# Differential heads' halves in their own 64 rows, scores in three products of 64 rows each

## The chip, the core and the metric

The kernel runs on one core of one Trainium2 chip. The metric is the device time of one execution in microseconds (us); the time of before is the median of three runs. The profile is one further execution, recorded by the hardware profiler. Engines are named as in the profile: PE is TensorE's matrix products and PEld its weight loads, DVE is VectorE, ACT ScalarE, POOL GpSimd, and SP SyncE, which issues most transfers.

## What is computed

Two layers of a mixer with three head groups in parallel. The part that the change touches is the scores of group D, differential attention: 6 heads, each with two halves of 64 dimensions, whose softmaxes are subtracted. Cut to that:

```python
SEQ, DIFF_HEADS, DIFF_HALF_DIM, DIFF_V_DIM = 256, 6, 64, 128
...
h = rmsnorm(x, norm_g[l])
proj = h @ w_in[l]
a_x, a_b, a_c, a_g, d_q, d_k, d_v, d_g, m_q, m_g = jnp.split(proj, offsets, axis=-1)
...
q = rmsnorm(d_q.reshape(b, s, DIFF_HEADS, 2, DIFF_HALF_DIM), diff_q_norm_g[l])
k = rmsnorm(d_k.reshape(b, s, DIFF_HEADS, 2, DIFF_HALF_DIM), diff_k_norm_g[l])
...
sc = jnp.einsum('bhcqd,bhckd->bhcqk', qi, kt).astype(jnp.float32) * scale + bias[None, :, None]
p = jax.nn.softmax(sc, axis=-1).astype(vt.dtype)
o = jnp.einsum('bhcqk,bhkd->bhcqd', p, vt)
return o[:, :, 0] - lam.astype(o.dtype) * o[:, :, 1]
...
x = x + jnp.concatenate([y_a, y_d, y_m], axis=-1) @ w_out[l]
```

All inputs and the output are float32.

## The kernel before

Precision first. A large product is made of three products in fp32r: each operand is split into an upper part `hi` (rounded to fp32r) and a lower part `lo` (the rest), and hi·hi, hi·lo and lo·hi are summed in PSUM (L304, L305, L306). Weights come in by transfers of 128 × 1024 (`raw`), ACT makes `hi` (L283), and DVE makes `lo` (L284). The activations of a layer, 256 tokens, stand with the dimension on the 128 rows, in `xT` for the input projection and in `yT` for the output projection; `yT` has 2 parts × 16 slices of 256 tokens, and its slices are also used, before the output projection needs them, for queries and keys.

A layer is a row of blocks: `block` (L287 on) runs over 16 slices of the contraction in chunks of two, for 512 columns and two groups of 128 tokens, so a chunk has 12 products of 512 columns. After each chunk `run_side` moves forward the other work of the layer: tasks, written as generators, that fall due by chunk numbers. The attention's heads run there, in pairs (`pair`), one pair every nine chunks. Which instruction stands where on an engine follows from this program order and from a planner that simulates the engines when the program is built; `pin` (`keep_in_program_order`) holds the written order for an instruction.

A head of group D goes through these steps. `normed` normalizes queries and keys by token; `turn_sheet` transposes them (by 32 × 32 blocks on DVE, then through DRAM), so that `whole` has for each head a slice of 256 tokens with its first half in rows 0 to 63 and the second in rows 64 to 127. `qk_T` (from L457) splits them. For each half `c`, `own` are its own 64 rows and `other` the other 64:

- the query slice of a half, `yT[:, c, h]`, gets the upper part in `own` (L469) and the lower part in `other` (L470);
- the first key slice gets the upper part in both (L481, L482); the second gets the lower part in `own` (L486) and a copy of it in `other` (L488). For heads 4 and 5 this second slice lies in a tile of its own, `k2`.

So one product of 128 rows (L544) sums hi·hi and lo·hi, and a second (L545) sums hi·lo and lo·lo. `diff_scores` (from L537) makes 8 products of 256 columns a head: two halves, two groups of 128 queries, two products. The two halves' scores go to two PSUM tiles, `s[0]` and `s[1]`; the pool `ps_s` has two buffers. DVE reads them at L549 (adding the distance bias), then come the maximum (L551), the exponential on ACT (L555), and the difference of both halves (L562). Group M's scores (`mem_scores`, L590) and the products of probabilities with values (`weighted`, L437) are f32 products of 128 rows.

Two more instructions on PE matter below. Small vectors are turned at the start: `va` (32 rows, L817) and `vb` (64 rows, L145), each by one transposition between products of the memory projection (L738). Token blocks `xs` are turned by transpositions of 128 rows (L716), two at a time.

Of the kernel before, what the change touches and what calls it, by code (L numbers as in the profile page):

```python
# [11 lines left out]
F32 = mybir.dt.float32  # L12
# [36 lines left out]
def encoder(ctx: ExitStack, tc: tile.TileContext, x, mem, norm_g, w_in, conv_w, conv_b,  # L49
# [21 lines left out]
    def nm(s):  # L71
        uid[0] += 1
        return f"{s}_{uid[0]}"
# [369 lines left out]

    def q_parts(yT, c, h):
        return yT[:, c, h, :]

    def k_first(yT, c, h):
        return yT[:, c, CG + h, :]  # L450

    def k_second(yT, k2, c, h):
        return yT[:, c, CG + DH + h, :] if h < 4 else k2[:, c, h - 4, :]

    ROWS = (slice(0, HALF), slice(HALF, P))

    def qk_T(l, yT, k2, nat, q, k):  # L457

        whole = yield from turn_sheet(nat)

        pin = tc.keep_in_program_order
        if q is not None:
            c0, h0, nh = q
            a = c0 // P
            for c in range(2):
                own, other = ROWS[c], ROWS[1 - c]
                src = whole[own, a:a + nh, :]
                hi = yT[own, c, h0:h0 + nh, :]
                pin(nc.scalar.copy(hi, src))  # L469
                pin(nc.vector.tensor_tensor(yT[other, c, h0:h0 + nh, :], src, hi.bitcast(F32), ALU.subtract))  # L470
                yield
            made.update(("q", l, h) for h in range(h0, h0 + nh))
        if k is not None:
            c0, h0, nh = k
            a = c0 // P
            for c in range(2):
                own, other = ROWS[c], ROWS[1 - c]
                src = whole[own, a:a + nh, :]
                g = kgain[own, l:l + 1]
                hi = yT[own, c, CG + h0:CG + h0 + nh, :]  # L480
                pin(nc.scalar.activation(hi, src, AF.Copy, scale=g))  # L481
                pin(nc.scalar.activation(yT[other, c, CG + h0:CG + h0 + nh, :], src, AF.Copy, scale=g))  # L482
                for at, n, dst, d0 in ((0, min(nh, 4 - h0), yT, CG + DH + h0), (4 - h0, h0 + nh - 4, k2, 0)):
                    if n > 0:
                        lo = dst[own, c, d0:d0 + n, :]
                        pin(nc.vector.scalar_tensor_tensor(lo, whole[own, a + at:a + at + n, :], g,  # L486
                                                           hi[:, at:at + n].bitcast(F32), ALU.mult, ALU.subtract))
                        pin(nc.scalar.copy(dst[other, c, d0:d0 + n, :], lo))  # L488
                yield
            made.update(("k", l, h) for h in range(h0, h0 + nh))  # L490

    scored = set()
# [3 lines left out]
    def pair(heads, begin, end, v):  # L496

        es = []
        for h in heads:
            while held["e"] == 2:  # L500
                yield 1
            held["e"] += 1
            es.append((yield from begin(h)))
            yield 2
        yield 4
        while held["sh"] == 2:
            yield 1
        held["sh"] += 1
        sh = tmp.tile([P, NA, 2, NT * NT, B], F32, tag="sh", name=nm("sh"))
        for i, e in enumerate(es):  # L510
            tc.keep_in_program_order(nc.vector.transpose(
                sh[:, :, i], e[0].rearrange("p t (k b c) -> p b (t k) c", k=NT, b=NA)))
            held["e"] -= 1
            yield 1
        yield 4
        flat = sh.rearrange("p b h n c -> p (b h n c)")
        yield from carry(sh.rearrange("p b h n c -> p b (h n c)"), flat.rearrange("p (n a i) -> p n a i", a=NA, i=B))
        eT = flat.rearrange("p (h t k q) -> p h t k q", h=2, t=NT, k=NT)
        while held["yn"] == 2:
            yield 1  # L520
        held["yn"] += 1
        yn = tmp.tile([P, NA, 2, NT, B], F32, tag="yn", name=nm("yn"))
        for i, h in enumerate(heads):
            end[0](h, yn[:, :, i], weighted(eT, i, v, h), *es[i][1:])
            yield 2
        held["sh"] -= 1
        yield 5
        tc.keep_in_program_order(nc.vector.transpose(yn, yn))
        yield 5
        flat = yn.rearrange("p b h t c -> p (b h t c)")  # L530
        yield from carry(yn.rearrange("p b h t c -> p b (h t c)"), flat.rearrange("p (n a i) -> p n a i", a=NA, i=B))
        for i, h in enumerate(heads):
            end[1](h, flat[:, i * SEQ:(i + 1) * SEQ])
            yield 1
        held["yn"] -= 1

    def diff_scores(l, h, yT, k2):  # L537
        while not {("q", l, h), ("k", l, h)} <= made:
            yield 1
        s = [ps_s.tile([P, NT, SEQ], F32, tag="s", name=nm("s")) for _ in range(2)]  # L540
        for c in range(2):
            for i in range(NT):
                qi = q_parts(yT, c, h)[:, i * P:(i + 1) * P]
                nc.tensor.matmul(s[c][:, i, :], qi, k_first(yT, c, h), start=True, stop=False)  # L544
                nc.tensor.matmul(s[c][:, i, :], qi, k_second(yT, k2, c, h), start=False, stop=True)  # L545
        scored.add((l, h))
        e = tmp.tile([P, 2, NT, SEQ], F32, tag="e", name=nm("e"))
        for c in range(2):
            nc.vector.scalar_tensor_tensor(e[:, c], dist, -slopes[h], s[c], ALU.mult, ALU.add)  # L549
        mx = small.tile([P, 2, NT], F32, tag="mx", name=nm("mx"))  # L550
        nc.vector.tensor_reduce(mx, e, AX.X, ALU.max, negate=True)  # L551
        sm = small.tile([P, 2, NT], F32, tag="sm", name=nm("sm"))
        for c in range(2):
            for i in range(NT):
                nc.scalar.activation(e[:, c, i], e[:, c, i], AF.Exp, bias=mx[:, c, i:i + 1],  # L555
                                     accum_out=sm[:, c, i:i + 1])
        iv = small.tile([P, 2, NT], F32, tag="iv", name=nm("iv"), bufs=6)
        nc.vector.reciprocal(iv, sm)
        cf = small.tile([P, NT], F32, tag="cf", name=nm("cf"))
        nc.vector.scalar_tensor_tensor(cf, sm[:, 0], neglam[:, l:l + 1], iv[:, 1], ALU.mult, ALU.mult)  # L560
        for i in range(NT):
            nc.vector.scalar_tensor_tensor(e[:, 0, i], e[:, 1, i], cf[:, i:i + 1], e[:, 0, i], ALU.mult, ALU.add)  # L562
        return e[:, 0], iv
        yield
# [285 lines left out]
    for l in range(DEPTH):  # L850
# [4 lines left out]


        yT = T_tile("yT")
        k2 = keep.tile([P, 2, DH - 4, SEQ], F32R, tag="bgT", name=nm("k2"))

        def x_block(cols, order=ALLK, **how):  # L860
            return block(xT, w_in[l], cols, order, rows=x_row_tiles, **how)
# [1 line left out]
        def begin_pair(n, p):  # L863
            tasks.append(later(p, max(1, start + PAIR_EVERY * n - chunk[0])))
# [4 lines left out]
        for b in order:  # L869
            if b in begun:  # L870
                acc = x_block([(C_D + b * NB, NB)], ALLK[-QT:], acc=begun[b])
            else:
                acc = x_block([(C_D + b * NB, NB)])
            if b == 3:
                v = keep.tile([P, NT, W_DIFF], F32, tag="v", name=nm("v"))
                ga = keep.tile([P, NT, W_DIFF], F32, tag="ga", name=nm("ga"))
            if b == 4:
                start = chunk[0]
                for n in range(DH // 2):
                    begin_pair(n, pair((2 * n, 2 * n + 1), lambda h: diff_scores(l, h, yT, k2),  # L880
                                       (lambda h, yn, po, iv: diff_out(h, yn, po, iv, st, ga),
                                        lambda h, y: split_T(yT, CG + h, y, hgain[:, l:l + 1], pin=True)), v))
            if b < 3:
                tasks.append(later(qk_T(l, yT, k2, normed(acc, HALF, st, sheets(("mqT", "mga", "e")[b])),
                                 (0, 0, 4) if b == 0 else (0, 4, 2) if b == 1 else None,
                                 (256, 0, 2) if b == 1 else (0, 2, 4) if b == 2 else None), 8))
            else:
                for t in range(NT):
                    if b == 3:
                        nc.scalar.activation(v[:, t, 0:NB], acc[t], AF.Copy, scale=col(st, R, t))  # L890
                    elif b == 4:
                        nc.scalar.activation(v[:, t, NB:768], acc[t][:, 0:256], AF.Copy, scale=col(st, R, t))
                        silu2(ga[:, t, 0:256], acc[t][:, 256:512], st, t)
                    else:
                        silu2(ga[:, t, 256:768], acc[t], st, t)
# [149 lines left out]
```

## Time and profile before

| what | value |
|---|---|
| median of three runs | 924.12 us (924.11 to 926.16) |
| profiled execution | 924.1 us |
| its span, first to last instruction | 922.3 us |
| granted TensorE clock | 1.0 |
| PE busy | 917.0 us in 4176 records |
| DVE busy | 669.4 us in 1179 instructions |
| ACT busy | 495.0 us in 754 instructions |
| transfers | 215.06 MB, 233 GB/s |

In a row of the groups stand the line of the kernel, the engine, the operation, the tile written and the tiles read, the shapes and the count; then the busy time, the mean of one in ns, and the idle time just ahead of it with what ended it. In the order of time a row begins with the start and the duration in us; rows that follow on one another are merged (x2), with idle time ahead of them in brackets. A product's recorded duration is the time from its first column's entry to its modelled end, longer than the distance from its start to the next one's. An f32 product of group M or of probabilities with values has two records.

### The profile page before, as it was taken

To read this page: it belongs to the slowest core of one execution; us is meant where nothing else is said; L and a number is where in the kernel's file an instruction comes from. 1 tells how busy PE (TensorE), PEld (TensorE's weight loads), DVE (VectorE), ACT (ScalarE), POOL (GpSimd) and SP (SyncE) were. 2 spreads that over 40 slices of the span, in tenths; PEclk is the share of its full clock that TensorE was granted. 3 is DMA by queue.
4 is the path that set the end of the run, shared out by engine and by line. 5 is a ranking of instruction groups with operands and counts; after the bars stand their busy time and mean duration, and the time that the engine had idled before them with its cause. 6 is when DMAs were issued, how large, how long until landed. Compare 5 with 4: busy or idle time off the path is not lost.

```text
span 922.3 us, 12258 instructions
## 1 busy us (share of the span) xinstructions
PE 917.0 (99%) x4176; PEld 761.0 (83%) x4176; DVE 669.4 (73%) x1179; ACT 495.0 (54%) x754; POOL 7.0 (1%) x18
## 2 busy tenths in 40 slices
PE   9999999999999999999999999999999999999998
PEld 6888888888888888888888888888888888888886
DVE  5797877857898786567676757878898776558652
ACT  6676645675545554445555544568554554446431
POOL 0001000000000000000000000000000000000000
PEclk9999999999999999999999999999999999999999
DMA  8998878876679999978687867986889889988662
GB/s 273 279 251 299 273 226 234 257 208 197 175 223 251 223 268 251 277 235 246 214 265 233 247 190 224 235 233 180 240 230 238 254 212 259 244 239 241 208 221 74
DMA packets 250498, 215.06 MB, mean 233 GB/s; under 512 B 131438, under 2 KB 177092, under 8 KB 250436
## 3 DMA queue, kind: packets, MB, share of 16 engines
q1 hardware_dynamic: 248004, 210.72, 80.3%
q0 software_dynamic: 672, 2.10, 0.7%
q10 hardware_dynamic: 1760, 1.46, 0.5%
q8 instruction: 33, 0.54, 0.2%
q14 instruction: 29, 0.24, 0.1%
HBM read 193.26 MB, written 20.97 MB: 232 GB/s over the span
## 4 chain that ended last, share of the span: by engine, by line
PE 99%; DMA 0%; ACTq 0%; ACT 0%; DVE 0%; DVEq 0%; issue 0%
PE acc L304 28%; PE acc L305 28%; PE acc L306 28%; PE acc L738 10%; PE po L437 2%; PE s L590 1%; PE s L545 1%; PE s L544 1%; DMA raw<-in_w_mem_kv_dram 0%; PE pt L716 0%; ACT hi L710 0%; ACTq L792 0%; DVE xs L1006 0%; DVEq L1040 0%; PE pvb L145 0%
## 5 line engine op out<-in xcount | busy, mean ns | idle before, releaser
L283 ACT CAST hi<-raw 128x1024 fp32r<-128x1024 f32 x288 | 302.7, 1052 | 347.0 <-PE acc L306 292.4
L284 DVE TENSOR_TENSOR lo<-raw,hi 128x1024 fp32r<-128x1024 f32 x288 | 351.8, 1222 | 185.8 <-ACT hi L283 179.7
L304 PE MATMUL acc<-hi,xT 128*128 128x512 f32 x896 | 350.3, 392 | 0.0
L305 PE MATMUL acc<-lo,xT 128*128 128x512 f32 x896 | 349.2, 390 | 0.0
L306 PE MATMUL acc<-hi,xT 128*128 128x512 f32 x896 | 348.9, 390 | 0.0
L306 PEld LDWEIGHTS acc<-hi,xT 128*128 128x128 f32 x896 | 168.2, 188 | 35.0
L304 PEld LDWEIGHTS acc<-hi,xT 128*128 128x128 f32 x896 | 168.3, 188 | 34.1
L305 PEld LDWEIGHTS acc<-lo,xT 128*128 128x128 f32 x896 | 168.3, 188 | 33.8
L306 PE MATMUL acc<-hi,yT 128*128 128x512 f32 x256 | 99.6, 389 | 0.0
L304 PE MATMUL acc<-hi,yT 128*128 128x512 f32 x256 | 99.6, 389 | 0.0
L305 PE MATMUL acc<-lo,yT 128*128 128x512 f32 x256 | 99.6, 389 | 0.0
L738 PE MATMUL acc<-hi,memT 128*128 128x512 f32 (+1 forms) x260 | 72.6, 393 | 0.6 <-ACT hi L710 0.6
L306 PEld LDWEIGHTS acc<-hi,yT 128*128 128x128 f32 x256 | 48.1, 188 | 10.1
L304 PEld LDWEIGHTS acc<-hi,yT 128*128 128x128 f32 x256 | 48.1, 188 | 9.9
L305 PEld LDWEIGHTS acc<-lo,yT 128*128 128x128 f32 x256 | 48.1, 188 | 9.9
L738 PEld LDWEIGHTS acc<-hi,memT 128*128 128x128 f32 x260 | 47.2, 188 | 10.2 <-ACT hi L710 1.0
L711 DVE SCALAR_TENSOR_TENSOR lo<-raw,cva,hi 128x1024 fp32r<-128x1024 f32 (+1 forms) x32 | 38.5, 1215 | 6.5 <-ACT hi L710 6.2
L738 PE MATMUL acc<-lo,memT 128*128 128x512 f32 (+1 forms) x130 | 39.9, 388 | 0.0
L710 ACT ACTIVATE hi<-raw,cva 128x1024 fp32r<-128x1024 f32 (+1 forms) x32 | 34.5, 1095 | 9.5 <-DMA raw<-in_w_mem_kv_dram 5.3
L738 PEld LDWEIGHTS acc<-lo,memT 128*128 128x128 f32 x130 | 24.3, 188 | 5.2
L555 ACT ACTIVATE e<-e,mx 128x256 f32<-128x256 f32 x48 | 23.8, 498 | 1.4 <-DVE mx L551 1.3
L549 DVE SCALAR_TENSOR_TENSOR e<-dist,s 128x512 f32<-128x512 f32 x24 | 15.7, 679 | 2.3 <-PE s L545 1.9
(149 smaller groups left out, 596.6 us busy)
## 6 DMA issues: line engine op xcount, KB each, us to landing
raw<-in_w_in_dram SPq DMA_DIRECT2D x192, 512.0 KB, 4.5
raw<-in_w_out_dram SPq DMA_DIRECT2D x64, 512.0 KB, 3.7
raw<-in_w_in_dram SPq DMA_DIRECT2D x64, 256.0 KB, 4.8
raw<-in_w_mem_kv_dram SPq DMA_DIRECT2D x30, 512.0 KB, 4.2
d<-sh SPq DMA_DIRECT2D x80, 128.0 KB, 4.1
sh<-d SPq DMA_DIRECT2D x64, 128.0 KB, 4.8
d<-yn SPq DMA_DIRECT2D x40, 64.0 KB, 4.0
yn<-d SPq DMA_DIRECT2D x40, 64.0 KB, 4.4
```

Source lines behind the costliest of these rows:

```text
L283: nc.scalar.copy(hi, raw)
L284: nc.vector.tensor_tensor(lo_, raw, hi.bitcast(F32), ALU.subtract)
L304: nc.tensor.matmul(acc[t], sh, hi, start=first, stop=False)
L305: nc.tensor.matmul(acc[t], sh, lo, start=False, stop=False)
L306: nc.tensor.matmul(acc[t], sl, hi, start=False, stop=last)
L437: nc.tensor.matmul(po[:, t, :], eT[:, i, t, k, :], v[:, k, h * P:(h + 1) * P], start=k == 0, stop=k == NT - 1)
L544: nc.tensor.matmul(s[c][:, i, :], qi, k_first(yT, c, h), start=True, stop=False)
L549: nc.vector.scalar_tensor_tensor(e[:, c], dist, -slopes[h], s[c], ALU.mult, ALU.add)
L555: nc.scalar.activation(e[:, c, i], e[:, c, i], AF.Exp, bias=mx[:, c, i:i + 1], accum_out=sm[:, c, i:i + 1])
L710: pin(nc.scalar.activation(hi, raw, AF.Copy, scale=gain))
L711: pin(nc.vector.scalar_tensor_tensor(lo, raw, gain, hi.bitcast(F32), ALU.mult, ALU.subtract))
L738: pin(nc.tensor.matmul(accs[l, half][t][:, at:at + n], memT[:, token_part, k, t * P:(t + 1) * P], p, start=k == 0 and at == 0 and token_pa ...
```

## The change

A head's query slice is now `yT[:, 0, h]` for the upper part and `yT[:, 1, h]` for the lower one, with both halves side by side as they stand in `whole`: the first in rows 0 to 63, the second in rows 64 to 127. Keys likewise, in slices `CG + h`. So one ACT instruction makes the upper parts of several heads and both halves, and one DVE instruction the lower parts; the copies into the other 64 rows, the second key slice and the tile `k2` are gone. The scores of a half are three products of its 64 rows, hi·hi, lo·hi and hi·lo (query part first); lo·lo is no longer in. The loop alternates between the halves, so a product of the upper rows into `s[0]` is followed by one of the lower rows into `s[1]`, and the products are pinned. A head has 2 × 3 × 2 = 12 of them.

```diff
-    def q_parts(yT, c, h):
-        return yT[:, c, h, :]
-
-    def k_first(yT, c, h):
-        return yT[:, c, CG + h, :]
-
-    def k_second(yT, k2, c, h):
-        return yT[:, c, CG + DH + h, :] if h < 4 else k2[:, c, h - 4, :]
-
     ROWS = (slice(0, HALF), slice(HALF, P))
 
-    def qk_T(l, yT, k2, nat, q, k):
+    def qk_T(l, yT, nat, q, k):
 
         whole = yield from turn_sheet(nat)
 
         pin = tc.keep_in_program_order
         if q is not None:
             c0, h0, nh = q
-            a = c0 // P
-            for c in range(2):
-                own, other = ROWS[c], ROWS[1 - c]
-                src = whole[own, a:a + nh, :]
-                hi = yT[own, c, h0:h0 + nh, :]
-                pin(nc.scalar.copy(hi, src))
-                pin(nc.vector.tensor_tensor(yT[other, c, h0:h0 + nh, :], src, hi.bitcast(F32), ALU.subtract))
-                yield
+            src = whole[:, c0 // P:c0 // P + nh, :]
+            hi, lo = (yT[:, part, h0:h0 + nh, :] for part in range(2))
+            pin(nc.scalar.copy(hi, src))
+            pin(nc.vector.tensor_tensor(lo, src, hi.bitcast(F32), ALU.subtract))
             made.update(("q", l, h) for h in range(h0, h0 + nh))
+            yield
         if k is not None:
             c0, h0, nh = k
-            a = c0 // P
-            for c in range(2):
-                own, other = ROWS[c], ROWS[1 - c]
-                src = whole[own, a:a + nh, :]
-                g = kgain[own, l:l + 1]
-                hi = yT[own, c, CG + h0:CG + h0 + nh, :]
-                pin(nc.scalar.activation(hi, src, AF.Copy, scale=g))
-                pin(nc.scalar.activation(yT[other, c, CG + h0:CG + h0 + nh, :], src, AF.Copy, scale=g))
-                for at, n, dst, d0 in ((0, min(nh, 4 - h0), yT, CG + DH + h0), (4 - h0, h0 + nh - 4, k2, 0)):
-                    if n > 0:
-                        lo = dst[own, c, d0:d0 + n, :]
-                        pin(nc.vector.scalar_tensor_tensor(lo, whole[own, a + at:a + at + n, :], g,
-                                                           hi[:, at:at + n].bitcast(F32), ALU.mult, ALU.subtract))
-                        pin(nc.scalar.copy(dst[other, c, d0:d0 + n, :], lo))
-                yield
+            src = whole[:, c0 // P:c0 // P + nh, :]
+            hi, lo = (yT[:, part, CG + h0:CG + h0 + nh, :] for part in range(2))
+            g = kgain[:, l:l + 1]
+            pin(nc.scalar.activation(hi, src, AF.Copy, scale=g))
+            pin(nc.vector.scalar_tensor_tensor(lo, src, g, hi.bitcast(F32), ALU.mult, ALU.subtract))
             made.update(("k", l, h) for h in range(h0, h0 + nh))
...
-        for c in range(2):
-            for i in range(NT):
-                qi = q_parts(yT, c, h)[:, i * P:(i + 1) * P]
-                nc.tensor.matmul(s[c][:, i, :], qi, k_first(yT, c, h), start=True, stop=False)
-                nc.tensor.matmul(s[c][:, i, :], qi, k_second(yT, k2, c, h), start=False, stop=True)
+        for i in range(NT):
+            for q_part, k_part in ((0, 0), (1, 0), (0, 1)):
+                for c in range(2):
+                    pin(nc.tensor.matmul(s[c][:, i, :], yT[ROWS[c], q_part, h, i * P:(i + 1) * P],
+                                         yT[ROWS[c], k_part, CG + h, :], start=q_part == k_part, stop=k_part == 1))
```

What this does to the order of instructions on TensorE is shown at two places. The names are the tile written, then the tiles read, each with its number in the program. The first place is the first head of layer 0. Before, its first product stands alone among products of the input projection (`acc`, `hi`, `lo`, `xT`), and the others follow ten rows later:

```order
L304 MATMUL acc_1958<-hi_1962,xT_108 128x512
L304 MATMUL acc_1959<-hi_1962,xT_108 128x512
L544 MATMUL s_1978<-yT_1038 128x256
L305 MATMUL acc_1958<-lo_1963,xT_108 128x512
L306 MATMUL acc_1958<-hi_1962,xT_108 128x512
```

Now all twelve stand together behind a chunk of the projection, the halves' tiles by turns:

```order
L305 MATMUL acc_1937<-lo_1942,xT_108 128x512
L306 MATMUL acc_1937<-hi_1941,xT_108 128x512
L304 MATMUL acc_1938<-hi_1941,xT_108 128x512
L305 MATMUL acc_1938<-lo_1942,xT_108 128x512
L306 MATMUL acc_1938<-hi_1941,xT_108 128x512
L522 MATMUL s_1957<-yT_1038 128x256
L522 MATMUL s_1958<-yT_1038 128x256
```

The rows behind these are the same two by turns, twelve products in all; what moved is that none of the twelve stands apart. The second place is the second head of the same pair. Before, its eight products stand together, `s_2040` first and then `s_2041`:

```order
L306 MATMUL acc_1958<-hi_2024,xT_108 128x512
L304 MATMUL acc_1959<-hi_2024,xT_108 128x512
L305 MATMUL acc_1959<-lo_2025,xT_108 128x512
L306 MATMUL acc_1959<-hi_2024,xT_108 128x512
L544 MATMUL s_2040<-yT_1038 128x256
L545 MATMUL s_2040<-yT_1038 128x256
```

Now its first product stands alone, with two products of the projection between it and the other eleven:

```order
L304 MATMUL acc_1937<-hi_2055,xT_108 128x512
L305 MATMUL acc_1937<-lo_2056,xT_108 128x512
L306 MATMUL acc_1937<-hi_2055,xT_108 128x512
L522 MATMUL s_2023<-yT_1038 128x256
L304 MATMUL acc_1938<-hi_2055,xT_108 128x512
L305 MATMUL acc_1938<-lo_2056,xT_108 128x512
L522 MATMUL s_2024<-yT_1038 128x256
```

All three pairs of both layers have this form, so the 144 score products of the changed kernel stand in 18 groups: six of twelve, six of one and six of eleven. Before, the 96 products stood in 15 groups.

More of the change, by code (lines that the diff above doesn't have):

```diff
@@ L535, in pair, with diff_scores @@
         held["yn"] -= 1
-    def diff_scores(l, h, yT, k2):
+    def diff_scores(l, h, yT):
         while not {("q", l, h), ("k", l, h)} <= made:
@@ L857, in encoder @@
         yT = T_tile("yT")
-        k2 = keep.tile([P, 2, DH - 4, SEQ], F32R, tag="bgT", name=nm("k2"))
         def x_block(cols, order=ALLK, **how):
@@ L879, in encoder @@
                 for n in range(DH // 2):
-                    begin_pair(n, pair((2 * n, 2 * n + 1), lambda h: diff_scores(l, h, yT, k2),
+                    begin_pair(n, pair((2 * n, 2 * n + 1), lambda h: diff_scores(l, h, yT),
                                        (lambda h, yn, po, iv: diff_out(h, yn, po, iv, st, ga),
@@ L883, in encoder @@
             if b < 3:
-                tasks.append(later(qk_T(l, yT, k2, normed(acc, HALF, st, sheets(("mqT", "mga", "e")[b])),
+                tasks.append(later(qk_T(l, yT, normed(acc, HALF, st, sheets(("mqT", "mga", "e")[b])),
                                  (0, 0, 4) if b == 0 else (0, 4, 2) if b == 1 else None,
```

## The prediction

> **What bounds the kernel now.** I read the page first, then the list of waits, then the matrix products in order of time. The page gives the span, each engine's busy time, the granted clock and the shares of the chain that ended last:
>
> ```profile
> span 922.3 us, 12258 instructions
> PE 917.0 (99%) x4176; PEld 761.0 (83%) x4176; DVE 669.4 (73%) x1179; ACT 495.0 (54%) x754; POOL 7.0 (1%) x18
> ...
> PEclk9999999999999999999999999999999999999999
> ...
> PE 99%; DMA 0%; ACTq 0%; ACT 0%; DVE 0%; DVEq 0%; issue 0%
> ```
>
> The reader is to see that TensorE (PE) carries 99% of the chain at an unchanged clock. A busy PE need not be a fast one, so the list of what PE and its weight loader waited for comes next; it has four rows for the loader, the longest in total 2.4 us (the warm-up products at the start), first of them here, and two for the products:
>
> ```profile
> PEld L122 <- issue: 2.4, 7, 0.8
> ```
>
> ```profile
> PE warm L122 <- PEq L1031: 0.8, 1, 0.8
> PE acc L738 <- ACT hi L710: 0.6, 1, 0.6
> ```
>
> So no product of the layers waits for VectorE (DVE), ScalarE (ACT) or a transfer, and the time is the sum of the slots that the products take, one behind another. A slot is the distance between two starts. The order of time gives it for products of 512 columns:
>
> ```profile
> 499.74 0.39 PE L304 MATMUL acc<-hi,yT 128*128 128x512 f32 x1
> ...
> 501.78 0.39 PE L304 MATMUL acc<-hi,yT 128*128 128x512 f32 x1
> ```
>
> Nine products lie between these starts: 2.04 / 9 = 0.227 us each. The recorded 0.39 us is how long one is in flight. And for the score products, of 256 columns:
>
> ```profile
> 209.27 0.28 PE L545 MATMUL s<-yT 128*128 128x256 f32 x1
> 209.38 0.28 PE L544 MATMUL s<-yT 128*128 128x256 f32 x1
> ...
> 209.98 0.28 PE L545 MATMUL s<-yT 128*128 128x256 f32 x1
> 210.10 0.40 PE L304 MATMUL acc<-hi,xT 128*128 128x512 f32 x1
> ```
>
> Seven slots from 209.27 to 210.10: 0.83 / 7 = 0.12 us each. Their number stands in the groups by shape:
>
> ```profile
> L544 PE MATMUL s<-yT 128*128 128x256 f32 x48 | 12.3, 286 | 0.0
> L545 PE MATMUL s<-yT 128*128 128x256 f32 x32 | 8.1, 283 | 0.0
> L545 PE MATMUL s<-k,yT 128*128 128x256 f32 x16 | 3.9, 280 | 0.0
> ```
>
> **The change, part by part.** First, what goes: 48 + 32 + 16 = 96 score products, at 0.12 us: 11.5 us of PE time, 1.25% of the span. This is all that PE can get back.
>
> Second, the score products that come. Twelve heads (six in each of two layers) times 12 products are 144, each of 256 columns and 64 rows. If an upper and a lower one run together, a pair takes one slot. The order of the changed program on TensorE puts them in 18 groups: six heads have all twelve together (six slots); in the other six, which are the second heads of their pairs, one product stands alone, then come two full-row products, then the other eleven (one slot, then six, since an odd one is left). That is 6 × 6 + 6 × 7 = 78 slots, 9.4 us. No row shows two products of 64 rows side by side, so their price is open between 0.06 us each (a slot per pair) and 0.12 us (a slot per product, 144 slots, 17.3 us). I take the pair, because two halves share neither rows nor a PSUM tile (`s[0]` and `s[1]`); the upper end stays for the range. On sharing, the Trainium skill, "TensorE: Matmul & The Clock Gate", Part 3: Packing small matmuls, says that products in different row groups run concurrently, each further one adding about 4 ns; by it 66 pairs would cost an estimated 0.3 us more than the sum takes, and no run here shows it.
>
> Third, the passage between products of 128 rows and products of fewer. The kernel before has two such places, the transposition of `vb` (64 rows, L145) and of `va` (32 rows, L817). First `vb`, products and weight loads in order of time:
>
> ```profile
> 87.44 0.39 PE L738 MATMUL acc<-lo,memT 128*128 128x512 f32 x1
> 87.75 0.13 PEld L145 LDWEIGHTS pvb<-ident,vb 64*128 64x128 f32 x1 [0.35 <-issue]
> 87.75 0.27 PE L145 MATMUL pvb<-ident,vb 64*128 64x64 f32 x1
> 87.95 0.19 PEld L738 LDWEIGHTS acc<-hi,memT 128*128 128x128 f32 x1
> 88.06 0.19 PEld L738 LDWEIGHTS acc<-hi,memT 128*128 128x128 f32 x1
> 88.29 0.39 PE L738 MATMUL acc<-hi,memT 128*128 128x512 f32 x1
> ```
>
> The weights of `vb` go in only 0.31 us after the start of the product ahead, though the profile shows nothing that they wait for ("issue"), and those of the next full-row product only 0.20 us after that. For comparison, a transposition of 128 rows, of the same type and also between full-row products:
>
> ```profile
> 7.72 0.39 PE L738 MATMUL acc<-hi,memT 128*128 128x512 f32 x1
> 7.72 0.14 PEld L716 LDWEIGHTS pt<-ident,xs 128*128 128x128 f32 x1
> 7.95 0.27 PE L716 MATMUL pt<-ident,xs 128*128 128x128 f32 x1
> 8.06 0.27 PE L716 MATMUL pt<-ident,xs 128*128 128x128 f32 x1
> 8.40 0.40 PE L738 MATMUL acc<-hi,memT 128*128 128x512 f32 x1
> ```
>
> Here the weights go in at the very start of the product ahead (7.72), and the way from 7.72 to 8.40, 0.68 us, is two slots of 0.227 and two transpositions of 0.11 each: no hold. With `vb` the way from 87.44 to 88.29 is 0.85 us: two slots of 0.227, a transposition of half the columns (0.06), and 0.34 left over. `va` gives the same:
>
> ```profile
> 7.00 0.28 PE L738 MATMUL acc<-lo,memT 128*128 128x256 f32 x1
> 7.20 0.14 PEld L817 LDWEIGHTS pva<-ident,va 32*128 32x128 f32 x1
> 7.38 0.19 PEld L738 LDWEIGHTS acc<-hi,memT 128*128 128x128 f32 x1
> ```
>
> From 7.00 to the second full-row product at 7.72: 0.72 − 0.12 − 0.23 − 0.03 = 0.34 us. So going to fewer rows and back costs about 0.34 us: twice the array is emptied first, and twice a weight load (0.11 us, 87.95 to 88.06) lies open. If a transposition's cost did not shrink with its columns (0.11), 0.29 and 0.26 would be left; built for score products from its parts, entry is 0.31 − 0.23 = 0.08 of hold and 0.11 of load, exit the same, about 0.38, say 0.40 at most. The outer end below is zero, since both rows are f32 transpositions and not fp32r products; I keep it as a rival. I take 0.34 for each of the 18 groups: 6.1 us (4.7 to 7.2).
>
> Fourth, ACT and DVE. The duplicates and the half-sheets go; per layer the heads' parts now take four ACT and four DVE instructions over 128 rows. Most of what goes away:
>
> ```profile
> L482 ACT ACTIVATE yT<-sh,kgain 64x1024 fp32r<-64x1024 f32 x4 | 4.6, 1150 | 0.1
> L482 ACT ACTIVATE yT<-sh,kgain 64x512 fp32r<-64x512 f32 x4 | 2.9, 723 | 0.1
> L488 ACT CAST yT<-yT 64x512 fp32r<-64x512 f32 x8 | 5.0, 620 | 0.2
> L488 ACT CAST k<-k 64x512 fp32r<-64x512 f32 x4 | 2.5, 614 | 0.0
> ```
>
> L482 and L488 alone are 4.6 + 2.9 + 5.0 + 2.5 = 15 us of ACT. I cost this at nothing: all of it lies beside PE, which waits for neither engine. It would count only if PE waited for a lower part of the weights in the stretch where the heads are prepared, and no such wait is listed. No transfer is added or taken away, and none is moved past another on SP's or POOL's queue.
>
> Fifth, a wait: the lone product of a second head needs the first PSUM tile of its pair's first head, read by DVE at L549:
>
> ```profile
> L549 DVE SCALAR_TENSOR_TENSOR e<-dist,s 128x512 f32<-128x512 f32 x24 | 15.7, 679 | 2.3 <-PE s L545 1.9
> ```
>
> Between the two groups lie 27 products, 27 × 0.227 = 6.1 us; the two reads take 0.68 us each. Behind the lone product stand the full-row products, but it has no cause to be late: nothing.
>
> The **sum**: 9.4 + 6.1 − 11.5 = +4.0 us, so the span becomes 926.3. The profiled execution took 924.1 us, 1.8 more than its span, and the median of the runs shown is 924.12, the same; so 928.1 us, 0.43% slower. With the bounds of the passage, +2.6 to +5.1: 926.7 to 929.2.
>
> **The rivals.** Each is a mechanism with its price; a difference under 0.3% (2.8 us) is about what a measurement of this kernel can't tell from no change.
>
> *The halves run one after another.* 144 slots: 17.3 + 6.1 − 11.5 = +11.9, 936.0 us; with 0.40 a passage, 937.1. For it: before, a weight load (0.11 us) fills nearly all of a 0.12 us slot, and if loads of both halves go through one after another, two products can't start in one slot. Against it: the halves lie in different rows. The Trainium skill, "TensorE: Matmul & The Clock Gate", LDWEIGHTS (loading the stationary operand), says that a load's time goes by its columns and not its rows; the trace agrees, 0.13 us for 64 rows (L145) and 0.14 for 128 (L716). By that rule loads in a queue would make this rival's sum.
>
> *No passage cost* (the other side: not slower). The hold belongs to f32 transpositions with few columns, not to a change of row count; weights of 64-row products then go in while the full-row product ahead runs. 9.4 − 11.5 = −2.1: 922.0 us, within 0.3%. It decides from a passage of 0.27 us down: 18 × 0.27 = 4.9, less 2.1, is +2.8. For it: no row shows an fp32r product of 64 rows. Against it: the 128-row transposition of the same type has no hold, and two places give the same 0.34.
>
> *The change doesn't do what it says, at no passage cost:* one slot per product, 17.3 − 11.5 = +5.8: 929.9 us.
>
> *Every change of half is held too.* In `vb`'s row one product of 64 rows, with its load and its emptying, takes 0.20 us (87.75 to 87.95); with 256 columns about 0.26. 144 × 0.26 = 37.4, plus 0.20 at 18 exits, less 11.5: +29.5, 953.6 us. No row speaks against it, as neither place has two halves. By the Trainium skill, "TensorEngine Tiling (Array Packing)", Key Properties, it would not occur: a change of mode drains the engine, a change of tile alone does not; no run here shows the second.
>
> **How the numbers follow.** Pairs with the passage 0.52; one after another with the passage 0.24; pairs without it 0.12; one after another without it 0.06; each half held 0.06. The predicted time is the first's, 928.1 us. The range leaves out the third and the last (0.18) and takes in the bounds of the others: from 924.8 (a passage of 0.16 us, below what the rows give, with pairs) to 937.2. Slower by over 0.3%: 0.44 of the first (the rest has a passage under 0.27), and the second, fourth and last, together 0.80. Within 0.3%: 0.08 of the first and 0.09 of the third, 0.17. Faster: 0.03 of the third, if pairs are shorter than a slot.
>
> **What would show it.** In the order of time of the changed kernel, at a group of L522: pairs of starts a few ns apart and 0.12 from pair to pair say that halves run together; even steps of 0.12 that they don't; steps near 0.26 that each is held. The weight load of a group's first product stands some 0.3 us behind the start of the full-row product ahead if there is a hold, at that start if not. Entry, twelve products and exit should take 6 × 0.12 + 0.34 = 1.06 us against 0.96 for eight before. PE should still wait for no one. A wait of PE for DVE or ACT in the new order, or a lone product that is late, would make the prediction wrong in a way that no case here has.

## The result, and the profile after

The changed kernel takes 930.13 us (median of four runs, 929.38 to 931.04) against 924.12 (four runs, 923.65 to 926.16): a ratio of 1.006, 95% interval 1.0048 to 1.0073. It is slower by 0.6%; the forecast was slower by 0.43%, 928.1 us. The page of its profiled execution (930.58 us, span 928.8):

```profile
span 928.8 us, 12308 instructions
...
PE 923.4 (99%) x4224; PEld 760.0 (82%) x4224; DVE 662.5 (71%) x1167; ACT 473.7 (51%) x726; POOL 7.0 (1%) x18
...
PE 99%; ACT 0%; ACTq 0%; DVE 0%; issue 0%; DVEq 0%
```

TensorE (PE) still makes up the chain. ACT has 21 us less to do and DVE 7, and the time is longer all the same. PE's busy time grew by 6.4 us with 48 products more.

What a group of twelve score products looks like is read from products and weight loads in order of time, the first head of layer 0:

```profile
210.24 0.39 PE L306 MATMUL acc<-hi,xT 128*128 128x512 f32 x1
210.56 0.39 PE L522 MATMUL s<-yT 64*128 64x256 f32 x2
210.56 0.19 PEld L522 LDWEIGHTS s<-yT 64*128 64x128 f32 x2 [0.35 <-issue]
210.78 0.40 PE L522 MATMUL s<-yT 64*128 64x256 f32 x4
211.02 0.40 PE L522 MATMUL s<-yT 64*128 64x256 f32 x4
211.25 0.28 PE L522 MATMUL s<-yT 64*128 64x256 f32 x2
211.46 0.19 PEld L304 LDWEIGHTS acc<-hi,xT 128*128 128x128 f32 x1
211.57 0.19 PEld L305 LDWEIGHTS acc<-lo,xT 128*128 128x128 f32 x1
211.80 0.40 PE L305 MATMUL acc<-lo,xT 128*128 128x512 f32 x1
```

Four things are to be seen. The first two products, an upper and a lower one, begin in the same hundredth of a us, and so do their weight loads: the halves run together. The loads begin 0.32 us after the start of the full-row product ahead, where a full-row load begins with it (210.02, with the product at 210.01). The second pair begins 0.22 us after the first and not 0.12, since the first load lay open (the product's recorded start is that of its load); from there to the last pair it is four steps in 0.47 us, 0.12 each. Behind the last pair (211.25) the next full-row load waits 0.21 us, and lies open for another 0.11 (211.46 to 211.57). From 210.24 to 211.80 it is 1.56 us; two slots of 0.227 and six of 0.12 leave **0.39 us for the passage**. A lone product, from the same view:

```profile
217.53 0.39 PE L306 MATMUL acc<-hi,xT 128*128 128x512 f32 x1
217.85 0.38 PE L522 MATMUL s<-yT 64*128 64x256 f32 x1
218.16 0.50 PE L304 MATMUL acc<-hi,xT 128*128 128x512 f32 x1
218.49 0.40 PE L305 MATMUL acc<-lo,xT 128*128 128x512 f32 x1
```

From 217.53 to 218.49, 0.96 − 0.45 − 0.12 = 0.39 again: one product pays as much as twelve. The list of waits shows the holds at entry (waiter, what ended it, us in all, times, longest):

```profile
PEld s L522 <- issue: 2.9, 8, 0.4
...
PEld s L522 <- DVE iv L536: 1.4, 4, 0.4
...
PEld s L522 <- DVE rsa L196: 0.7, 2, 0.4
PEld s L522 <- DVE lo L284: 0.7, 2, 0.4
```

Sixteen of the 18 entries are here, each some 0.36 us, and all alike whether the row names "issue" or a DVE instruction. So the DVE rows hardly name a cause: a wait for DVE would not be expected to have the same length each time. (The two groups that follow products with the values, L437, are not listed.)

How much of the 6 us is the scores? The first product of the input projection and the last of all, before (first two rows) and after:

```profile
97.61 0.39 PE L304 MATMUL acc<-hi,xT 128*128 128x512 f32 x1
...
917.99 0.39 PE L306 MATMUL acc<-hi,yT 128*128 128x512 f32 x1
```

```profile
98.95 0.39 PE L304 MATMUL acc<-hi,xT 128*128 128x512 f32 x1
...
924.44 0.39 PE L306 MATMUL acc<-hi,yT 128*128 128x512 f32 x1
```

Between them 820.4 us before and 825.5 after: **5.1 us belong to the layers**. The other 1.3 us lie ahead of them, in the memory projection, whose code the change doesn't touch. There the products of 256 columns run at another pace, before (first) and after:

```profile
6.64 0.40 PE L738 MATMUL acc<-hi,memT 128*128 128x256 f32 x2
6.88 0.40 PE L738 MATMUL acc<-lo,memT 128*128 128x256 f32 x2
```

```profile
7.24 0.63 PE L716 MATMUL acc<-hi,memT 128*128 128x256 f32 x2
7.67 0.63 PE L716 MATMUL acc<-lo,memT 128*128 128x256 f32 x2
```

Two in 0.24 us, against two in 0.43: TensorE is still slow at the start, some 3.5 us longer than before. (The granted clock reads 1.00 at this stage in both traces, so that it is the clock is not shown.) Which of the two it is changes from run to run of one and the same kernel. Six later runs of the changed kernel fall into 929.1 to 929.2 and 930.7 to 931.1, and eleven of the kernel before, taken beside them, into 923.9 to 924.5 and 925.7 to 926.0. That these sets are the two starts is read from all ten traces: where the profiled run belongs to the upper set, the input projection begins after 98.9 us, and where it belongs to the lower one, before 98. Like against like, the means differ by 5.0 us in both sets, as in the layers. So from here on each kernel is also given the time from the first product of the input projection to the last product, which leaves the start out. (The Trainium skill, "TensorE: Matmul & The Clock Gate", Part 1, says that the clock is released by a window of 3.4 us that runs freely and does not begin with the kernel, and that the ramp varies by run; that fits these rows, and no run here tests it.)

### The profile page after: what moved, and what is told of

It is laid out like the page before. It is cut to its first block, busy times and chain, and to the rows that moved or that the text cites. A ratio compares the mean times of both kernels' runs of the same rounds, so it can differ in the third digit from the quotient of the medians.

```text
span 928.8 us, 12308 instructions
## 1 busy us (share of the span) xinstructions
PE 923.4 (99%) x4224; PEld 760.0 (82%) x4224; DVE 662.5 (71%) x1167; ACT 473.7 (51%) x726; POOL 7.0 (1%) x18
## 4 chain that ended last, share of the span: by engine, by line
PE 99%; ACT 0%; ACTq 0%; DVE 0%; issue 0%; DVEq 0%
PE acc L304 28%; PE acc L306 28%; PE acc L305 28%; PE acc L716 10%; PE po L437 2%; PE s L522 1%; PE s L568 1%; PE pt L694 0%; ACT L83 0%; ACTq L680 0%; ACT hi L688 0%; ACTq L770 0%; ACTq L773 0%; DVE xs L983 0%; DVEq L1017 0%
## 5 line engine op out<-in xcount | busy, mean ns | idle before, releaser
L399 DVE STREAM_TRANSPOSE sh<-sh 128x1024 f32<-128x1024 f32 (+2 forms) x14 | 17.3, 1238 | 0.0
```

What stands on the lines that cost most here:

```text
L399: tc.keep_in_program_order(nc.vector.transpose(src, src))
```

## The experiments

Every kernel below is the changed kernel with one edit. The theory: pairs of halves share a slot of 0.12 us, and each passage to 64 rows and back costs 0.386 us (from the 1.56 above, read to the ns). The rivals differ by run.

**The changed kernel again**, unaltered.

> The changed kernel once more, as the measure for the others. Theory: halves run in pairs at 0.12 us a pair, and each of the 18 passages to 64 rows and back costs 0.386 us (read from the trace of after: 1.56 us from the full-row product ahead of a group of twelve to the second one behind it, less two slots of 0.227 and six of 0.12), so the scores cost 16.4 us against 11.6 before: about 929 us, 5 more than before. Rival: some 1.3 us of the difference lie in the memory projection at the start, whose code did not change, and come and go between executions; then this repeat's first product of the input projection starts anywhere between 97.5 and 99 us.

929.92 us, ratio 1.0055 (1.0042 to 1.0067); in the layers 825.5 us, to the last digit as in the first execution. Its input projection began at 99.06 us, so this trace too has the long start; that the start is at other times short is seen in the run times alone. Both statements hold: the layers lose 5.1 us in both traces, the start some 1.3 us or nothing.

**Twelve groups instead of 18**, by pinning the large products.

```diff
-            nc.tensor.matmul(acc[t], sh, hi, start=first, stop=False)
+            pin(nc.tensor.matmul(acc[t], sh, hi, start=first, stop=False))
...
```

> The large products are pinned, so that every head's twelve score products stand in one group: 12 groups, not 18. Theory (price per passage): each lone product with its passage costs 0.509 us and a group of eleven 1.115, a group of twelve 1.106, so 6 x (0.509 + 1.115 - 1.106) = 3.1 us less than the changed kernel, about 926.5 to 927. Rival (the loss has nothing to do with the number of passages): the time of the changed kernel, about 930.

930.18 us, ratio 1.0059 (1.0046 to 1.0073); in the layers 824.9 us. By the total, the rival; but the trace shows twelve groups of 1.56 us each, as the theory had it, and a new wait:

```profile
PE po L437 <- DMA sh<-d: 1.8, 2, 1.1
```

```profile
PEld po L437 <- issue: 2.6, 2, 1.5
```

The products with the values of one pair in each layer now stood ahead of their sheet's return from DRAM. If the 3.1 us came, some 2.5 went into this wait. The run alone doesn't settle it.

**Pinned only while heads are scored**, so that the order elsewhere stays free.

```diff
+    scoring = [False]
+
+    def hold(i):
+        if scoring[0]:
+            tc.keep_in_program_order(i)
...
-            nc.tensor.matmul(acc[t], sh, hi, start=first, stop=False)
+            hold(nc.tensor.matmul(acc[t], sh, hi, start=first, stop=False))
...
+            scoring[0] = scoring[0] and len(scored) % DH > 0
...
+                scoring[0] = True
```

> The large products are pinned only while heads of group D are being scored, so that there are 12 groups of twelve as in the pinned kernel, but not the two waits of the products with the values (L437) for the sheet from DRAM, 0.9 and 1.3 us, that appeared in it. Theory: 12 x 1.106 = 13.3 us for the scores, 3.1 less than the changed kernel and 1.7 more than before: 822.4 us from the first product of the input projection to the last product, and 926 to 927 in all. Rival (those waits come with fewer passages, not with pinning, because the sheets are then due sooner): the same two waits, 824.6.

927.8 us, ratio 1.0026 (1.0016 to 1.0036); in the layers 822.6 us, where the theory said 822.4 and the rival 824.6. The total lies above the 926 to 927 that were expected; its profiled run had the long start (99.06 us). The list of waits has no row for the products with the values (L443 in this kernel). So the number of groups is worth what was said, and the pinning of all large products had made the wait.

**Six products of one half, then six of the other.**

```diff
-        for i in range(NT):
-            for q_part, k_part in ((0, 0), (1, 0), (0, 1)):
-                for c in range(2):
+        for c in (1, 0):
+            for i in range(NT):
+                for q_part, k_part in ((0, 0), (1, 0), (0, 1)):
```

> Six products of the lower half, then six of the upper, so that no two halves lie side by side but at the change: 12 groups. Theory (pairs share a slot): each product takes its own slot of 0.12, 12 x (12 x 0.12 + 0.386) = 21.9 us for the scores, 5.5 more than the changed kernel, about 935. Rival (alternating gives nothing, and only the number of groups counts): 12 groups as in the pinned kernel, about 927. Second rival (a change of half is held too): 12 x 0.2 to 0.3 us more than the theory, about 938.

930.84 us, ratio 1.0067 (1.0055 to 1.0079); in the layers 826.8 us. None of the three numbers. The first group in order of time:

```profile
208.88 0.39 PE L306 MATMUL acc<-hi,xT 128*128 128x512 f32 x1
209.20 0.38 PE L522 MATMUL s<-yT 64*128 64x256 f32 x1
209.43 0.51 PE L522 MATMUL s<-yT 64*128 64x256 f32 x3
209.55 0.18 PEld L522 LDWEIGHTS s<-yT 64*128 64x128 f32 x2
209.66 0.52 PE L522 MATMUL s<-yT 64*128 64x256 f32 x5
210.01 0.52 PE L522 MATMUL s<-yT 64*128 64x256 f32 x3
210.46 0.50 PE L304 MATMUL acc<-hi,xT 128*128 128x512 f32 x1
210.79 0.40 PE L305 MATMUL acc<-lo,xT 128*128 128x512 f32 x1
```

From 208.88 to 210.79 it is 1.91 us: without two full slots and the passage, 1.07 us, nine slots and not twelve. The row of weight loads tells why. After three products (209.20, 209.43, 209.55) two loads begin together, one of them for the other half, whose first product is the seventh in program order and starts at 209.55 too. From there two trains with steps of about 0.118 us run side by side. The records do not name the half, but they name the products that signal DVE: of the twelve only those that start at 209.90 and 210.25 do, and in program order these are the sixth and the twelfth, the last of each half. The one at 209.90 is the ninth to start, so three products of the second half went ahead of it. Why the second train begins after three products is open. The run confirms that halves share the array, even when they are not written by turns; it contradicts my assumption that TensorE would take them up in written order, and alternating is worth less than I had said, three slots a head.

**The same twelve products over all 128 rows.** In this kernel and the next two the second half of a pair also comes first (`c in (1, 0)`).

```diff
-                for c in range(2):
-                    pin(nc.tensor.matmul(s[c][:, i, :], yT[ROWS[c], q_part, h, i * P:(i + 1) * P],
-                                         yT[ROWS[c], k_part, CG + h, :], start=q_part == k_part, stop=k_part == 1))
+                for c in (1, 0):
+                    pin(nc.tensor.matmul(s[c][:, i, :], yT[:, q_part, h, i * P:(i + 1) * P],
+                                         yT[:, k_part, CG + h, :], start=q_part == k_part, stop=k_part == 1))
```

> The twelve products in the same places, but over all 128 rows, so both halves' scores are sums over both halves, and not the reference's. No passage and no pairs. Theory: 144 slots of 0.12 = 17.3 us against 16.4 for the changed kernel, so about 1 us more than it, 930 to 931; the way from the product ahead of a group of twelve to the second one behind it is 12 x 0.12 + 2 x 0.227 = 1.9 us. Rival (the array is emptied at the score products whatever their rows): 18 x 0.39 = 7 us more, about 937.

931.31 us, ratio 1.0067 (1.0055 to 1.008); in the layers 826.2 us. A group in the place of the one above:

```profile
210.35 0.39 PE L306 MATMUL acc<-hi,xT 128*128 128x512 f32 x1
210.58 1.59 PE L522 MATMUL s<-yT 128*128 128x256 f32 x12
212.01 0.40 PE L304 MATMUL acc<-hi,xT 128*128 128x512 f32 x1
212.24 0.40 PE L305 MATMUL acc<-lo,xT 128*128 128x512 f32 x1
```

1.89 us, twelve slots and two full ones, and no hold: the first score product comes 0.23 us after the product ahead. So the hold belongs to the 64 rows, not to the score products or their place. By the sum, pairs save 66 slots, 7.9 us, of which the passages take back 6.9; the layers of the changed kernel are 0.7 us shorter than these.

**The light preparation alone**, with 8 products of 128 rows.

```diff
-            for q_part, k_part in ((0, 0), (1, 0), (0, 1)):
-                for c in range(2):
-                    pin(nc.tensor.matmul(s[c][:, i, :], yT[ROWS[c], q_part, h, i * P:(i + 1) * P],
-                                         yT[ROWS[c], k_part, CG + h, :], start=q_part == k_part, stop=k_part == 1))
+            for k_part in range(2):
+                for c in (1, 0):
+                    pin(nc.tensor.matmul(s[c][:, i, :], yT[:, 0, h, i * P:(i + 1) * P],
+                                         yT[:, k_part, CG + h, :], start=k_part == 0, stop=k_part == 1))
```

> The light preparation of the change, but the scores as 8 products of 128 rows a head, as many and as long as before; each sums over both halves, so the scores are not the reference's. Theory (only TensorE's slots count, and the 22 us that ACT and the 7 us that DVE have less to do are hidden): the same time as before within 0.3%, 924 to 926; from the first product of the input projection to the last product of all 820.4 us as before, against 825.5 in the changed kernel. Rival (the light preparation is worth something, and the change's loss at TensorE is larger than the 5 us seen): 2 us or more below before.

925.48 us against 924.57 for the kernel before, run beside it; ratio 1.0002 (0.9992 to 1.0011); in the layers 820.5 us against 820.4. The relief of ACT and DVE is worth nothing here, as costed. Against the twelve full-row products of the kernel above, 48 products fewer make the layers 5.7 us shorter, 0.119 us each.

**More groups**: a head's two query groups in two chunks.

```diff
-                for c in range(2):
+                for c in (1, 0):
...
                                          yT[ROWS[c], k_part, CG + h, :], start=q_part == k_part, stop=k_part == 1))
+            if i == 0:
+                yield 1
```

> A head's two query groups in two chunks, six products each: 26 groups in place of 18, with 74 slots of pairs in place of 78. Theory (a passage costs 0.386 us): 26 x 0.386 + 74 x 0.12 = 18.9 us for the scores against 16.4 in the changed kernel, so 2.5 more: 828.0 us from the first product of the input projection to the last product, against 825.5. Rival (the passage's price goes by the products in the group, not by the group): 825.0, half a us less, since four slots fewer are needed.

931.6 us, ratio 1.007 (1.0057 to 1.0082); in the layers 828.0 us, the theory's number. A group of six:

```profile
218.46 0.39 PE L306 MATMUL acc<-hi,xT 128*128 128x512 f32 x1
218.78 0.62 PE L522 MATMUL s<-yT 64*128 64x256 f32 x6
219.33 0.50 PE L304 MATMUL acc<-hi,xT 128*128 128x512 f32 x1
219.66 0.40 PE L305 MATMUL acc<-lo,xT 128*128 128x512 f32 x1
```

From 218.46 to 219.66, 1.20 − 0.45 − 0.36 = 0.39.

**Fewer groups**: both heads of a pair in one, 24 products.

```diff
-    ps_s = pool("ps_s", 2, PSUM)
-    ps_t = pool("ps_t", 2, PSUM)
+    ps_s = ps_t = pool("ps_s", 4, PSUM)
...
+        both = (h, h + 1) if h % 2 == 0 else ()
...
+        for g in both:
+            waiting[g] = [ps_s.tile([P, NT, SEQ], F32, tag="s", name=nm("s")) for _ in range(2)]
+        for g in both:
...
-            tasks.append(later(p, max(1, start + PAIR_EVERY * n - chunk[0])))
+            tasks.append(later(p, max(1, start + PAIR_EVERY * n + (6 if n == 2 else 0) - chunk[0])))
```

> Both heads of a pair are scored in one group of 24 products: 6 groups, not 18. Their four PSUM tiles come from one pool of four buffers that the transpositions and the products with the values share, and the third pair begins six chunks later. Theory (0.386 us a passage, 0.12 a pair of products): 6 x (0.386 + 12 x 0.12) = 11.0 us for the scores, 5.4 less than the changed kernel and 0.6 less than before: 820.1 us from the first product of the input projection to the last product, against 825.5 and 820.4, and about 924 to 925.5 in all, no measurable difference from before. Rival (TensorE now waits for a PSUM buffer or for the heads that begin later): 821 us or more, with a wait listed for it.

923.73 us, against 925.35 for the kernel before, run beside it (whose runs fell more often on the long start): ratio 0.9994, 0.9985 to 1.0003, no difference that can be told. Sorted by the two starts, the means are 923.4 against 924.0 and 925.1 against 925.5. In the layers 819.7 us, 0.7 under before; from the changed kernel's time 820.1 was expected, from the scores' sum 0.6 under before. No new wait is listed in the layers. A group:

```profile
209.24 0.39 PE L305 MATMUL acc<-hi,xT 128*128 128x512 f32 x1
209.56 1.69 PE L525 MATMUL s<-yT 64*128 64x256 f32 x24
211.18 0.50 PE L303 MATMUL acc<-hi,xT 128*128 128x512 f32 x1
211.51 0.40 PE L304 MATMUL acc<-lo,xT 128*128 128x512 f32 x1
```

From 209.24 to 211.51, 2.27 − 0.45 − 12 × 0.12 = 0.38. Together:

| kernel | groups | layers, us | ratio to before |
|---|---|---|---|
| before | – | 820.4 | 1 |
| light preparation, 8 full-row products | – | 820.5 | 1.0002 |
| two heads a group | 6 | 819.7 | 0.9994 |
| pinned while scoring | 12 | 822.6 | 1.0026 |
| pinned throughout, with the wait at L437 | 12 | 824.9 | 1.0059 |
| changed | 18 | 825.5 | 1.006 |
| more groups | 26 | 828.0 | 1.007 |
| half by half | 12 | 826.8 | 1.0067 |
| 12 full-row products | – | 826.2 | 1.0067 |

From 6 to 26 groups (6, 12, 18, 26), with 72, 72, 78 and 74 slots of pairs, the layers' time goes with the groups: less 0.12 us a slot it is 811.1, 814.0, 816.1 and 819.1, and 20 groups more cost 8.0 us, 0.40 a group. The steps between neighbours are not even, 0.36 to 0.48 a group; the kernel with 6 groups also differs in its PSUM pools and in when the third pair begins. The kernel before, with 96 slots and no group of 64 rows, comes to 808.9 by the same sum, 0.39 a group below the one with 26.

## Why the prediction was right, and where it was off

- **The bound.** TensorE's slots alone set the time; the light preparation alone left it where it was (1.0002). Right, and with it the cost of nothing for ACT and DVE.
- **What goes**, 96 slots, 11.5 us. Right: between the kernels with 12 and with 8 full-row products a head, a slot is worth 0.119 us in the layers' time.
- **What comes**, 78 slots for 144 products. Right: the first two products and their loads start together, and pairs follow at 0.12 us. The rival in which halves run one after another is out, and so is its fellow without a passage cost.
- **The passage.** Mechanism and place right, the size too small: I took 0.34 us from `vb` and `va`, and it is 0.386, inside the bounds of 0.26 to 0.40 that I gave. The way from the parts (hold and open load on each side, 0.38) was the better one; that the load and the emptying of the small f32 transpositions are not those of a score product is the likely reason, and no run tests it. Over 18 groups that is 0.8 us of the miss.
- **No passage cost** is out: twelve full-row products in the same places show no hold, and 0.39 us goes with every group. **Each half held** is out: the step between pairs is 0.12 us, not 0.26.
- **The lone product's wait**, costed at nothing: right; its 0.39 us is the passage and not a wait for DVE, though the list of waits names DVE for some.
- **The sum.** +4.0 us forecast, +5.1 in the layers: 0.8 for the passage, and a little more because groups of eleven take 1.57 us (218.49 to 220.06), which leaves 0.40 for theirs. Some 0.2 stay open. The full-row products behind a group take more than 0.227 us (211.80 to 212.04, 0.24), but they did so before the change too (210.10 to 210.34).
- **The total.** The medians lie 6.0 us apart, beyond the +2.6 to +5.1 that the bounds of the passage gave. The likely reason is the start: of the four runs of each kernel two fell on the long one with the change and one before it. The prediction had no term for it, and that its range still held 930.13 us is owed to the room that it left for the rivals.

## What to carry to other kernels

In these runs two products that use half the rows each do run together on TensorE, but a stream of full-row products pays 0.39 us each time it passes to half rows and back. With slots of 0.12 us a passage costs more than three slots, so here 12 products of 64 rows (six slots) lose to 8 of 128 rows, while with 24 in one group they come out 0.7 us ahead in the layers, too little for the medians of the total to tell. Count the passages in the built order, not in the source: the planner had made 18 of 12.

## What the runs showed that was not expected

TensorE took up the other half's products ahead of earlier ones of the first half: in the half-by-half kernel the second train began 0.35 us after the first, when three of its six products had started. The price of the passage was the same for 1, 6, 12 and 24 products. And 1.3 to 1.9 us of a run hang on when TensorE comes up to speed at the start (the input projection begins at 97.61 us before, at 98.95 in the changed kernel and at 99.47 with the light preparation alone), a quarter to over a third of the 5.1 us that were to be measured.
